# Lag kernels of four state-space groups on four column parts of TensorE at once, lag zero from b and c themselves, and an earlier bank copy in the MLP

## The chip, the cores and the metric

The kernel runs on one core of a Trainium2 chip (trn2). A core has five engines that work side by side and wait for each other through semaphores: TensorE (PE; its weight loads are shown as a lane of their own, PEld), VectorE (DVE), ScalarE (ACT), GpSimd (POOL) and SyncE (SP), which issues most of the DMA transfers. TensorE writes to PSUM, which has eight banks; VectorE and ScalarE read the banks and so give them back.

The metric is the device time of one execution in microseconds; a kernel's number is the median over several runs. Matmul clock is given as a share of full speed ("granted clock").

## The reference

The reference is one encoder layer on two sequences of 512 tokens with 1024 features:

```
h    = rms_norm(x, ln1);  q, k, v, u, g_att, g_ssm = split(h @ w_in)
y    = windowed attention(q, k, v)
s    = S5(u): 64 groups of 16 channels, 64 complex states per group, two directions
       bu_t = B_bar u_t;  h_t = A_bar h_(t-1) + bu_t;  out_t = Re(C h_t) + d_skip * u_t
s    = gelu(s) * sigmoid(gelu(s) @ w_glu + b_glu)
x    = x + (sigmoid(g_att) * y + sigmoid(g_ssm) * s) @ w_out
out  = x + relu(rms_norm(x, ln2) @ w_up)^2 @ w_down
```

The change touches the S5 branch and the first products of the last line. In S5 the effect of `u` at one token on the output `n` tokens later (a lag of `n`) is the 16x16 matrix Re(C A_bar^n B_bar) of its group; the other direction has the same with negative lags, and lag zero is the sum of both directions plus the diagonal `d_skip`.

## The kernel before

All the large products are made in a split form: each 32-bit operand is cut into a high part (a cast on ScalarE) and a low part (a subtraction on VectorE), and three matmuls stand for one (`mm3`, L114 to L118). The kernel goes through these stages: the projection of `u` and the gates, the S5 tables (this change), a scan over chunks of eight tokens on VectorE, the reading out of S5, attention, the GLU and the output product, the up product of the MLP and the down product of the MLP. The MLP uses seven products of half-size blocks in place of eight.

**The table stage** is the loop `for q in range(NQ4)` (L720 to L746): 16 turns, each for four groups (`SG = 4`); two turns share the operands of eight groups (`SB = 8`). The order of PE, ACT, DVE and SP here is written out by hand (`manual_schedule`, opened at L270), so each engine goes through its instructions as the Python code issues them. A turn issues:

- `coefficients` (L602, in odd turns, for the next two): small VectorE products that make `bb` (B_bar) and two planes for each of `bb` and `cx` (C).
- `lags_out(q - 1)` (L702) and `table_out(q)` (L656): DMA issues on SP. The lag kernels go to `lag_scr` in memory.
- `turn(q, gp)` (L664): four transposes of `bpre` on TensorE into a `tps` bank, and ScalarE's copy `bm` of them; two of these.
- `lag_weights` (L624, in even turns after the first): three ScalarE copies of `bb` into `lbt`, 48 columns a group: 16 for the forward direction, 16 for the backward one, 16 for both.
- `tables(q + 1)` (L647): six VectorE instructions: `complex_table` (L630) makes `bpre` with eight powers and `ctab` with nine (index 8 is the power zero).
- `run(3)`: three steps of a gate's or a column's product on TensorE, nine matmuls of 512 columns ("acc").
- `states(q, gp)` (L672): four matmuls into an `sps` bank, and two ScalarE copies of it into `h`; two of these, with the SP loads `inputs_in` for the next turn.
- `lags(q)` (L684): the lag kernels. Eight calls of TensorE: for each of four groups a real and an imaginary one, 48 columns of weights from `lbt`, 144 moving columns from `ctab` (nine lags of 16 channels). Two groups stand at partitions 0 and 64 of the `lag` bank. ScalarE copies the two halves out (`ks`, L695); GpSimd makes `dg`, a diagonal of `d_skip`, and adds it to lag zero (L698, L700).
- `run(3)` again, nine more matmuls, and what is owed to ScalarE and VectorE from the steps.

After the loop GpSimd's queue spreads `lag_scr` into `toep_scr` (L749), which is loaded again near the end of the scan, and the scan starts (L879), with the rest of the gates' products on TensorE beside it.

**The entry of the MLP** (L1875 to L1948) is also ordered by hand on PE, ACT, DVE and POOL. Four half products of the first two row pairs are made before the front's PSUM pools are closed; the third and fourth are `p1` and `p2` at L1904 and L1905, in two `acc` banks. `first_copy` (L1842) copies `p1` to `u1` on ScalarE, `first_rest` (L1850) adds `p2` to it on VectorE. After `front.close()` the pool `ps_m` takes over all eight banks, and each of its tiles waits for what used its bank before (`reuse_waits="tile"`). Its first product is `p6` of row pair 0, with the operands `made[2]` and `T2`; then come `p7` (`made[3]`, `T3`), `p5` (`made[1]`, `T1`), `p3` (`made[4]`, `B22`) and `p4`. From there on the order is made by the framework's planner, except in the last row pair.

```
    p1 = product(acc(), first[1][0], B11)
    p2 = product(acc(), first[1][1], B21)
    x22c = last.temp("x22")
    S.copy(x22c, x22)
...
    begun[0] = rest0()
    u1 = first_copy(p1)
```

Of the kernel before, what the change touches and what calls it, by code (L numbers as in the profile page):

```python
# [24 lines left out]
KT = D // P  # L25
# [15 lines left out]
CH = 16  # L41
# [23 lines left out]
def hybrid_layer(ctx, tc, x, xT, rel, onehot, early, w_qkv, w_ug, q_gain, k_gain, sink,  # L65
# [26 lines left out]
    y2_scr = dram.tile([GROUPS, CH, T, NSEQ * NCHUNK], F32, name="y2_scr")  # L92
    ct_scr = dram.tile([P, GROUPS // SG, 2, SG, 9 * CH], F32, name="ct_scr")
    toep_scr = dram.tile([T, CH, GROUPS, T * CH], F32, name="toep_scr")
# [89 lines left out]
    cf = coef_cm.__enter__()  # L184
    e2 = cf.tile([P, 9, GROUPS // SG, 2, SG], F32, name="e2")
    b2 = cf.tile([P, T, GROUPS // SG, 2, SG], F32, name="b2")
    e_s = cf.tile([P, 9, GROUPS], F32, name="e_s")
# [3 lines left out]
    dd = cf.tile([48, GROUPS], F32, name="dd")  # L191
    lbt = cf.tile([P, 2, SB, 48], F32, name="lbt")
    ssmb_cm = tc.tile_pool(name="ssmb", bufs=2)
# [79 lines left out]
    with tc.tile_pool(name="xin", bufs=2, reuse_waits="tile") as xin, tc.tile_pool(name="ssmc", bufs=1) as sc:  # L273
# [8 lines left out]
        V.memset(ones, 1.0)  # L282
        V.memset(lbt, 0.0)
        rows, columns, first_w = {}, {}, []

# [41 lines left out]
        bc_tiles = {0: b_and_c(0)}  # L327
        SP.dma_start(dd[32:48, :], d_skip)
        SP.dma_start(bglu_sb, b_glu)
# [215 lines left out]
        for pl, src in ((1, pr), (0, pi)):  # L545
            sv = src.rearrange("p n (q g) -> p n q g", g=SG)
            S.copy(e2[0:64, 0:8, :, pl], sv[0:64, 1:9])
            S.copy(e2[64:128, 0:8, :, pl], sv[64:128, 8:0:-1])
            S.copy(e2[:, 8, :, pl], sv[:, 0])
            S.copy(b2[0:64, :, :, pl], sv[0:64, 7::-1])  # L550
            S.copy(b2[64:128, :, :, pl], sv[64:128, 0:8])
# [43 lines left out]
    if True:  # L595
# [3 lines left out]
        with tc.tile_pool(name="ssmt", bufs=2) as sp:  # L599
            coefs, made, u_in, turned, lag_ks = {}, {}, {}, {}, {}  # L600

# [22 lines left out]
            def lag_weights(c):  # L624
                bb = coefs[c][0]
                S.copy(lbt[0:64, :, :, 0:16], bb[0:64])
                S.copy(lbt[64:128, :, :, 16:32], bb[64:128])
                S.copy(lbt[:, :, :, 32:48], bb)

            def complex_table(out, q, powers, total, planes, first, n):  # L630

                g0, ql = q * SG, slice(q % 2 * SG, (q % 2 + 1) * SG)
                V.tensor_mul(out.rearrange("p r g n c -> p (r g) n c"),
                             powers[:, 0:n, q].rearrange("p n r g -> p (r g) n")[:, :, :, None]
                             .to_broadcast([P, 2 * SG, n, CH]),
                             planes[:, q % 2].rearrange("p r g c -> p (r g) c")[:, :, None, :]
                             .to_broadcast([P, 2 * SG, n, CH]))
                tb = sp.tile([P, SG, 9, CH], F32, tag="tb", name="tb", bufs=1)
# [6 lines left out]
                V.tensor_add(ov, ov, tv[:, None].to_broadcast([P, 2, SG, n * CH]))  # L645

            def tables(q):  # L647

                bb, bk, cx, ck = coefs[q // 2]
                bpre = sp.tile([P, 2, SG, T, CH], F32, tag="bpre", name="bpre", bufs=1)  # L650
                complex_table(bpre, q, b2, b_s, bk, bb[:, 0], T)
                ctab = sp.tile([P, 2, SG, 9, CH], F32, tag="ctab", name="ctab")
                complex_table(ctab, q, e2, e_s, ck, cx[:, 0], 9)
                made[q] = bpre, ctab
# [29 lines left out]
            def lags(q):  # L684
                ks = lag_ks[q] = sp.tile([48, SG, 9, CH], F32, tag="ks", name="ks", bufs=1)
                ctab = made[q][1]
                ps = ps_o.tile([P, 512], F32, tag="po", name="lag")
                for g in range(SH):
                    for ri in range(2):
                        for e in range(2):  # L690
                            i = e * SH + g
                            PE.matmul(ps[e * 64:e * 64 + 48, g * 144:(g + 1) * 144], lbt[:, ri, q % 2 * SG + i, :],  # L692
                                      ctab[:, ri, i].rearrange("p n c -> p (n c)"), start=ri == 0, stop=ri == 1)
                for e in range(2):
                    S.copy(ks[:, e * SH:(e + 1) * SH].rearrange("p g n c -> p (g n c)"), ps[e * 64:e * 64 + 48, 0:SH * 144])  # L695
                g0 = q * SG
                dg = sp.tile([48, SG, CH], F32, tag="dg", name="dg", bufs=1)
                GP.tensor_tensor(dg[32:48], dd[32:48, g0:g0 + SG, None].to_broadcast([16, SG, CH]),  # L698
                                 ident[32:48, None, 32:48].to_broadcast([16, SG, CH]), op=ALU.mult)
                GP.tensor_tensor(ks[32:48, :, 8, :], ks[32:48, :, 8, :], dg[32:48], op=ALU.add)  # L700

            def lags_out(q):  # L702
                ks, gl = lag_ks.pop(q), slice(q * SG, (q + 1) * SG)
                SP.dma_start(lag_scr[:, gl, 8:15, :], ks[0:16, :, 0:7, :])
                SP.dma_start(lag_scr[:, gl, 0:7, :], ks[16:32, :, 1:8, :])
                SP.dma_start(lag_scr[:, gl, 7, :], ks[32:48, :, 8, :])

# [146 lines left out]
    with tc.tile_pool(name="ssmo", bufs=2, reuse_waits="tile") as sp:  # L854
# [54 lines left out]
        def tables_in(q):  # L909
# [5 lines left out]
            SP.dma_start(toep, toep_scr[:, :, g0:g0 + SH].rearrange("t c g n -> (t c) g n"))  # L915
            ctab = sp.tile([P, 2, SH, 9 * CH], F32, tag="ctab", name="ctab_in", bufs=5)
            SP.dma_start(ctab, ct_scr[:, q // 2, :, q % 2 * SH:(q % 2 + 1) * SH, :])
# [924 lines left out]
    def first_copy(p1):  # L1842
        u1 = up1.tile([P, HALF], F32, tag="u1", name="u1")
        S.copy(u1, p1)  # L1844
        return u1
# [60 lines left out]
    x22c = last.temp("x22")  # L1906
    S.copy(x22c, x22)
    V.tensor_sub(sm[2], a11_, a21_)
    V.tensor_sub(last.s11, x22c, x12)
# [9 lines left out]
    begun[0] = rest0()  # L1919
    u1 = first_copy(p1)  # L1920
    last.old_rows(1)
# [235 lines left out]
def layout(inputs):  # L2157
# [3 lines left out]
    def cols(w, n=CB):  # L2161
# [21 lines left out]
        "c_im": a["c_im"][0].transpose(0, 3, 1, 2).reshape(P, GROUPS, CH),  # L2183
        "d_skip": a["d_skip"][0].reshape(GROUPS, CH).T,
        "w_glu": cols(a["w_glu"][0], P),
# [25 lines left out]
```

## Time and profile before

| what | value |
|---|---|
| median of 3 runs | 1455.46 us (1453.98 to 1455.81) |
| the profiled execution | 1454.6 us, of which 1452.6 us are the span of its instructions |
| PE busy | 1438.1 us (99% of the span), 7768 matmul records |
| PEld / DVE / ACT / POOL busy | 85% / 75% / 54% / 13% of the span |
| granted clock of TensorE | 0.999 over the span |

The page of the profile lists busy times, the span in 40 slices, the DMA queues, the chain that ended last and the costliest groups. A 32-bit matmul call that is not in split form leaves two records in the trace, so the eight calls of `lags` are 16 records. Matmuls are pipelined: a record's duration overlaps its neighbour's, and what one costs is read from the distance of starts.

### The profile page before, as it was taken

Reading aid. Unit: us, or ns where it says so; the run is one execution under the profiler, and the core shown is the slowest. Engines: PE = TensorE matmul, PEld = TensorE weight load, DVE = VectorE, ACT = ScalarE, POOL = GpSimd, SP = SyncE. Lnnn points to the kernel's source line nnn. Section 1 sums busy time; section 2 is a strip of 40 time slices with the busy share of each in tenths; the row PEclk is TensorE's granted clock in tenths of the full one; section 3 lists DMA queues with packets and bytes.
Section 4 is the critical chain, followed back from the end, with each engine's and each line's share of the span. In section 5 each row is a group of like instructions: output and inputs, shape, how many; then the busy total and the mean of one; then the engine's idle time right before and its main releaser. Section 6 shows DMA issues by size and latency. Waiting matters only on the chain.

```text
span 1452.6 us, 21571 instructions
## 1 busy us (share of the span) xinstructions
PE 1438.1 (99%) x7768; PEld 1230.4 (85%) x7768; DVE 1086.3 (75%) x1853; ACT 782.8 (54%) x1404; POOL 182.7 (13%) x259
## 2 busy tenths in 40 slices
PE   9999999999999999999999989999999999999998
PEld 7888888889999999988888878888888888888887
DVE  8799979975637999987854897777776588475654
ACT  7788862233427999896432455554554434333332
POOL 2011120000223555471001000000000000000000
PEclk9999999999999999999999999999999999999999
DMA  8455567359922443356852334544443994464441
GB/s 307 124 168 174 165 207 266 103 173 302 300 88 64 120 123 104 110 190 221 264 175 92 133 116 160 159 142 140 153 149 121 332 326 133 157 192 143 128 131 58
DMA packets 130134, 243.86 MB, mean 168 GB/s; under 512 B 16059, under 2 KB 59323, under 8 KB 130028
## 3 DMA queue, kind: packets, MB, share of 16 engines
q1 hardware_dynamic: 105740, 187.39, 41.0%
q10 hardware_dynamic: 21888, 46.15, 8.4%
q0 software_dynamic: 2400, 8.95, 1.8%
q8 instruction: 61, 1.00, 0.3%
q14 instruction: 45, 0.37, 0.1%
HBM read 173.20 MB, written 81.82 MB: 176 GB/s over the span
## 4 chain that ended last, share of the span: by engine, by line
PE 93%; DVE 3%; ACT 1%; DMA 1%; issue 1%; SPq 0%; POOL 0%; ACTq 0%; DVEq 0%
PE bank L117 13%; PE bank L118 13%; PE bank L116 13%; PE acc L142 12%; PE acc L797 9%; PE acc L835 5%; PE acc L116 3%; PE acc L118 3%; PE acc L117 3%; PE po L1172 3%; PE sps L1140 2%; PE tps L1156 2%; PE sps L677 2%; PE sps L942 2%; PE lag L692 1%; PE sps L940 1%
## 5 line engine op out<-in xcount | busy, mean ns | idle before, releaser
L117 PE MATMUL bank<-b_lo,a_hi 128*128 128x512 f32 x440 | 171.4, 390 | 0.5 <-DVE b_lo L2085 0.5
L116 PE MATMUL bank<-b_hi,a_hi 128*128 128x512 f32 x440 | 171.2, 389 | 0.0
L118 PE MATMUL bank<-b_hi,a_lo 128*128 128x512 f32 x440 | 171.2, 389 | 0.0
L2084 ACT CAST a_hi<-d_a 128x1024 fp32r<-128x1024 f32 x55 | 58.0, 1054 | 177.5 <-PE bank L117 176.2
L2085 DVE TENSOR_TENSOR a_lo<-d_a,a_hi 128x1024 fp32r<-128x1024 f32 x55 | 67.2, 1222 | 98.6 <-ACT a_hi L2084 96.5
L116 PE MATMUL bank<-act,u_hi 128*128 128x512 f32 x256 | 100.3, 392 | 4.7 <-ACT u L1844 4.7
L117 PE MATMUL bank<-act,u_hi 128*128 128x512 f32 x256 | 100.3, 392 | 0.0
L118 PE MATMUL bank<-act,u_lo 128*128 128x512 f32 x256 | 100.2, 391 | 0.0
L117 PEld LDWEIGHTS bank<-b_lo,a_hi 128*128 128x128 f32 x440 | 82.6, 188 | 18.4 <-DVE b_lo L2085 1.2
L118 PEld LDWEIGHTS bank<-b_hi,a_lo 128*128 128x128 f32 x440 | 82.6, 188 | 17.2
L116 PEld LDWEIGHTS bank<-b_hi,a_hi 128*128 128x128 f32 x440 | 82.6, 188 | 17.1
L797 PE MATMUL acc<-w_hi,hT 128*128 128x256 f32 x384 | 84.4, 293 | 0.0
L797 PE MATMUL acc<-w_hi,act 128*128 128x256 f32 x384 | 81.2, 290 | 0.0
L142 PE MATMUL acc<-act,c_hi 128*128 128x512 f32 x256 | 80.6, 395 | 0.0
L142 PE MATMUL acc<-hT,c_hi 128*128 128x512 f32 x256 | 80.5, 394 | 0.0
L1150 ACT ACTIVATE p<-p,nmx 128x257 f32<-128x257 f32 (+1 forms) x128 | 72.0, 564 | 13.0 <-DVE nmx L1144 12.3
L1868 ACT CAST u_hi<-s 128x512 fp32r<-128x512 f32 x64 | 39.7, 622 | 67.2 <-PE bank L117 44.7
L1144 DVE CUSTOM_DVE_ANT_0 p<-sps,bias,nsink 128x256 f32<-128x256 f32 (+1 forms) x128 | 69.3, 542 | 4.4 <-PE sps L1140 2.9
L2085 DVE TENSOR_TENSOR b_lo<-k,b_hi 128x1024 fp32r<-128x1024 f32 x55 | 67.0, 1217 | 0.0
L797 PEld LDWEIGHTS acc<-w_hi,hT 128*128 128x128 f32 x384 | 63.8, 190 | 0.9
L797 PEld LDWEIGHTS acc<-w_hi,act 128*128 128x128 f32 x384 | 63.1, 190 | 0.8
L116 PEld LDWEIGHTS bank<-act,u_hi 128*128 128x128 f32 x256 | 48.5, 189 | 15.2 <-ACT u L1844 5.2
(415 smaller groups left out, 3963.5 us busy)
## 6 DMA issues: line engine op xcount, KB each, us to landing
d_a<-a_scr SPq DMA_DIRECT2D x55, 512.0 KB, 3.6
u_raw<-in_w_up_dram SPq DMA_DIRECT2D x32, 512.0 KB, 5.8
a_scr<-t ACTq DMA_DIRECT2D x64, 256.0 KB, 2.1
k<-in_w_down_dram SPq DMA_DIRECT2D x32, 512.0 KB, 5.8
a_scr<-a ACTq DMA_DIRECT2D x48, 256.0 KB, 3.2
c_raw<-in_w_ug_dram SPq DMA_DIRECT2D x44, 256.0 KB, 4.0
ct_scr<-ctab SPq DMA_DIRECT2D x16, 576.0 KB, 3.2
ctab_in<-ct_scr SPq DMA_DIRECT2D x32, 288.0 KB, 4.8
```

Source lines behind the costliest of these rows:

```text
L116: PE.matmul(ps, a[0], b[0], start=first, stop=False)
L117: PE.matmul(ps, a[0], b[1], start=False, stop=False)
L118: PE.matmul(ps, a[1], b[0], start=False, stop=last)
L142: PE.matmul(self.ps[s], self.w[p == 2][:, k, :], hT[s][p == 1][:, k, :], start=i % (3 * KT) == 0, stop=i % (3 * KT) == 3 * KT - 1)
L797: PE.matmul(ps, act[p == 2][:, k, col:col + P], self.w[k // 4][p == 1][:, k % 4, :], start=i == 0, stop=i == 3 * KT - 1)
L835: PE.matmul(self.ps[s], w_g[self.m][p == 2][:, k, :], y_part(s, int(p == 1), k), start=k + p == 0, stop=k == KT - 1 and p == 2)
L1144: V.tensor_tensor_reduce(self.p[:, h, 1:1 + self.nk], self.s[h][:, 0:self.nk], biases[self.j][h][:, b0:b0 + self.nk], -1.0, nsink[:, hh:hh ...
L1150: S.activation(p, p, AF.Exp, bias=self.nmx[:, h:h + 1], scale=-1.0, accum_out=self.sums[:, h, self.qb:self.qb + 1])
L1172: PE.matmul(self.po, vv, self.hl[i][part], start=i + part == 0, stop=i == self.nkb - 1 and part == 1)
L1868: S.copy(hi, src)
L2084: S.copy(hi, src)
L2085: V.tensor_sub(lo, src, hi.bitcast(F32))
```

## The change

Five things are changed.

1. The lag matmuls: `lbt` has 32 columns a group (forward and backward channels interleaved), `ctab` eight powers, so a call has 32 columns of weights and 128 moving columns. The four groups of a turn stand at partitions 0, 32, 64 and 96 of the bank, and the calls go through the four groups inside, real and imaginary part outside. It is eight calls a turn as before.
2. Lag zero: in even turns eight more calls, for all eight groups of two turns, two groups a call: weights `bz` (32 columns, `bb` in another order), 32 moving columns from `cx` and its negated imaginary part `ncx`. VectorE adds the diagonal in one instruction (`kz`), with a mask `same` that GpSimd makes at the start of the kernel and `d_skip` laid out over all partitions. GpSimd's two instructions a turn go.
3. The copies: one ScalarE copy of 128x128 a turn in place of two of 48x288; in `lag_weights` two copies of `bb` into `lbt`, one into `bz`, and the negation `ncx`, in place of three copies.
4. The DMAs: two a turn for the lag kernels, and two more in even turns for lag zero, in place of three a turn; `ct_scr` and its loads are one ninth smaller. `e2`, `e_s` and `ctab` have eight powers in place of nine, and two ScalarE copies into `e2` go.
5. The MLP's entry: `u1 = first_copy(p1)` for row pair 1 is issued right after the copy of `x22`, in place of after `begun[0] = rest0()`.

```diff
-    e2 = cf.tile([P, 9, GROUPS // SG, 2, SG], F32, name="e2")
+    e2 = cf.tile([P, T, GROUPS // SG, 2, SG], F32, name="e2")
...
-    lbt = cf.tile([P, 2, SB, 48], F32, name="lbt")
+    same = cf.tile([P, 32], F32, name="same")
+    lbt = cf.tile([P, 2, SB, 32], F32, name="lbt")
...
+        GP.tensor_tensor(same_v, eye[0], eye[1], op=ALU.add)
+        for n in (2, 3):
+            GP.tensor_tensor(same_v, same_v, eye[n], op=ALU.add)
...
             def lag_weights(c):
                 bb = coefs[c][0]
-                S.copy(lbt[0:64, :, :, 0:16], bb[0:64])
-                S.copy(lbt[64:128, :, :, 16:32], bb[64:128])
-                S.copy(lbt[:, :, :, 32:48], bb)
+                S.copy(lbt[0:64, :, :, 0::2], bb[0:64])
+                S.copy(lbt[64:128, :, :, 1::2], bb[64:128])
+                ncx = minus[c] = sp.tile([P, SB, CH], F32, tag="ncx", name="ncx", bufs=1)
+                S.activation(ncx, coefs[c][2][:, 1], AF.Copy, scale=-1.0)
+                bz = turned_bb[c] = sp.tile([P, 2, SB // 2, CH, 2], F32, tag="bz", name="bz", bufs=1)
+                S.copy(bz, bb.rearrange("p r (e g) c -> p r e c g", g=2))
...
-                complex_table(ctab, q, e2, e_s, ck, cx[:, 0], 9)
+                complex_table(ctab, q, e2, e_s, ck, cx[:, 0], T)
...
-                for g in range(SH):
-                    for ri in range(2):
-                        for e in range(2):
-                            i = e * SH + g
-                            PE.matmul(ps[e * 64:e * 64 + 48, g * 144:(g + 1) * 144], lbt[:, ri, q % 2 * SG + i, :],
-                                      ctab[:, ri, i].rearrange("p n c -> p (n c)"), start=ri == 0, stop=ri == 1)
-                for e in range(2):
-                    S.copy(ks[:, e * SH:(e + 1) * SH].rearrange("p g n c -> p (g n c)"), ps[e * 64:e * 64 + 48, 0:SH * 144])
...
-                GP.tensor_tensor(dg[32:48], dd[32:48, g0:g0 + SG, None].to_broadcast([16, SG, CH]),
-                                 ident[32:48, None, 32:48].to_broadcast([16, SG, CH]), op=ALU.mult)
-                GP.tensor_tensor(ks[32:48, :, 8, :], ks[32:48, :, 8, :], dg[32:48], op=ALU.add)
+                for ri in range(2):
+                    for e in range(SG):
+                        PE.matmul(ps[e * 32:(e + 1) * 32, 0:P], lbt[:, ri, q % 2 * SG + e, :],
+                                  ctab[:, ri, e].rearrange("p n c -> p (n c)"), start=ri == 0, stop=ri == 1)
+                if q % 2 == 0:
+                    bz, cx = turned_bb[q // 2], coefs[q // 2][2]
+                    for ri, c in enumerate((cx[:, 0], minus[q // 2])):
+                        for e in range(SG):
+                            two = slice(2 * e, 2 * e + 2)
+                            PE.matmul(ps[e * 32:(e + 1) * 32, P:P + 32], bz[:, ri, e].rearrange("p c g -> p (c g)"),
+                                      c[:, two].rearrange("p g c -> p (g c)"), start=ri == 0, stop=ri == 1)
+                S.copy(ks, ps[:, 0:P])
+                if q % 2 == 0:
+                    kz = zero[q] = sp.tile([P, 32], F32, tag="kz", name="kz", bufs=1)
+                    V.scalar_tensor_tensor(kz, same, dd[:, q // 2:q // 2 + 1], ps[:, P:P + 32], op0=ALU.mult, op1=ALU.add)
...
     x22c = last.temp("x22")
     S.copy(x22c, x22)
+    u1 = first_copy(p1)
     V.tensor_sub(sm[2], a11_, a21_)
...
     begun[0] = rest0()
-    u1 = first_copy(p1)
     last.old_rows(1)
```

More of the change, by code (lines that the diff above doesn't have):

```diff
@@ L92, in hybrid_layer @@
     y2_scr = dram.tile([GROUPS, CH, T, NSEQ * NCHUNK], F32, name="y2_scr")
-    ct_scr = dram.tile([P, GROUPS // SG, 2, SG, 9 * CH], F32, name="ct_scr")
+    ct_scr = dram.tile([P, GROUPS // SG, 2, SG, T * CH], F32, name="ct_scr")
     toep_scr = dram.tile([T, CH, GROUPS, T * CH], F32, name="toep_scr")
@@ L184, in hybrid_layer @@
     cf = coef_cm.__enter__()
-    e2 = cf.tile([P, 9, GROUPS // SG, 2, SG], F32, name="e2")
+    e2 = cf.tile([P, T, GROUPS // SG, 2, SG], F32, name="e2")
     b2 = cf.tile([P, T, GROUPS // SG, 2, SG], F32, name="b2")
-    e_s = cf.tile([P, 9, GROUPS], F32, name="e_s")
+    e_s = cf.tile([P, T, GROUPS], F32, name="e_s")
     b_s = cf.tile([P, T, GROUPS], F32, name="b_s")
@@ L190, in hybrid_layer @@
     fi = cf.tile([P, GROUPS], F32, name="fi")
-    dd = cf.tile([48, GROUPS], F32, name="dd")
-    lbt = cf.tile([P, 2, SB, 48], F32, name="lbt")
+    dd = cf.tile([P, KT], F32, name="dd")
+    same = cf.tile([P, 32], F32, name="same")
+    lbt = cf.tile([P, 2, SB, 32], F32, name="lbt")
     ssmb_cm = tc.tile_pool(name="ssmb", bufs=2)
@@ L283, in hybrid_layer @@
         V.memset(lbt, 0.0)
+        eye = [ident[:, n:n + 32].rearrange("p (c g) -> p c g", g=2) for n in range(0, P, 32)]
+        same_v = same.rearrange("p (g c) -> p c g", g=2)
+        GP.tensor_tensor(same_v, eye[0], eye[1], op=ALU.add)
+        for n in (2, 3):
+            GP.tensor_tensor(same_v, same_v, eye[n], op=ALU.add)
         rows, columns, first_w = {}, {}, []
@@ L327, in hybrid_layer @@
         bc_tiles = {0: b_and_c(0)}
-        SP.dma_start(dd[32:48, :], d_skip)
+        SP.dma_start(dd, d_skip)
         SP.dma_start(bglu_sb, b_glu)
@@ L546, in hybrid_layer @@
             sv = src.rearrange("p n (q g) -> p n q g", g=SG)
-            S.copy(e2[0:64, 0:8, :, pl], sv[0:64, 1:9])
-            S.copy(e2[64:128, 0:8, :, pl], sv[64:128, 8:0:-1])
-            S.copy(e2[:, 8, :, pl], sv[:, 0])
+            S.copy(e2[0:64, :, :, pl], sv[0:64, 1:9])
+            S.copy(e2[64:128, :, :, pl], sv[64:128, 8:0:-1])
             S.copy(b2[0:64, :, :, pl], sv[0:64, 7::-1])
@@ L599, in hybrid_layer @@
         with tc.tile_pool(name="ssmt", bufs=2) as sp:
-            coefs, made, u_in, turned, lag_ks = {}, {}, {}, {}, {}
+            coefs, minus, turned_bb, made, u_in, turned, lag_ks, zero = {}, {}, {}, {}, {}, {}, {}, {}
             def coefficients(c):
@@ L637, in complex_table @@
                              .to_broadcast([P, 2 * SG, n, CH]))
-                tb = sp.tile([P, SG, 9, CH], F32, tag="tb", name="tb", bufs=1)
+                tb = sp.tile([P, SG, T, CH], F32, tag="tb", name="tb", bufs=1)
                 V.tensor_mul(tb[:, :, 0:n, :],
@@ L651, in tables @@
                 complex_table(bpre, q, b2, b_s, bk, bb[:, 0], T)
-                ctab = sp.tile([P, 2, SG, 9, CH], F32, tag="ctab", name="ctab")
-                complex_table(ctab, q, e2, e_s, ck, cx[:, 0], 9)
+                ctab = sp.tile([P, 2, SG, T, CH], F32, tag="ctab", name="ctab")
+                complex_table(ctab, q, e2, e_s, ck, cx[:, 0], T)
                 made[q] = bpre, ctab
@@ L684, in lags @@
             def lags(q):
[L685 removed]
+                ks = lag_ks[q] = sp.tile([P, T * CH], F32, tag="ks", name="ks", bufs=1)
                 ctab = made[q][1]
                 ps = ps_o.tile([P, 512], F32, tag="po", name="lag")
[L688 to L693 removed]
@@ new lines, in lags @@
+                S.copy(ks, ps[:, 0:P])
+                if q % 2 == 0:
+                    kz = zero[q] = sp.tile([P, 32], F32, tag="kz", name="kz", bufs=1)
+                    V.scalar_tensor_tensor(kz, same, dd[:, q // 2:q // 2 + 1], ps[:, P:P + 32], op0=ALU.mult, op1=ALU.add)
+            def lags_out(q):
+                ks = lag_ks.pop(q)
+                for d, lag, n in ((0, 8, 0), (1, 0, CH)):
+                    SP.dma_start(lag_scr[:, q * SG:(q + 1) * SG, lag:lag + 7, :].rearrange("c g l n -> g c (l n)"),
+                                 ks[d::2, n:n + 7 * CH])
+                if q % 2 == 0:
+                    kz = zero.pop(q)
+                    for d in range(2):
+                        SP.dma_start(lag_scr[:, q * SG + d:q * SG + SB:2, 7, :].rearrange("c g n -> g c n"),
+                                     kz[d::2, d * CH:(d + 1) * CH])
@@ L915, in tables_in @@
             SP.dma_start(toep, toep_scr[:, :, g0:g0 + SH].rearrange("t c g n -> (t c) g n"))
-            ctab = sp.tile([P, 2, SH, 9 * CH], F32, tag="ctab", name="ctab_in", bufs=5)
+            ctab = sp.tile([P, 2, SH, T * CH], F32, tag="ctab", name="ctab_in", bufs=5)
             SP.dma_start(ctab, ct_scr[:, q // 2, :, q % 2 * SH:(q % 2 + 1) * SH, :])
@@ L2183, in layout @@
         "c_im": a["c_im"][0].transpose(0, 3, 1, 2).reshape(P, GROUPS, CH),
-        "d_skip": a["d_skip"][0].reshape(GROUPS, CH).T,
+        "d_skip": a["d_skip"][0].reshape(KT, 4, 2, CH).transpose(1, 3, 2, 0).reshape(P, KT),
         "w_glu": cols(a["w_glu"][0], P),
```

6 lines of the change are left out of this document (removed).

## The prediction

> **What bounds the kernel now**
>
> I read the page first, then who makes TensorE wait, then the two places that the change touches by stretches of time, by their chain and by single instructions. The page says which engine is full:
>
> ```profile
> PE 1438.1 (99%) x7768; PEld 1230.4 (85%) x7768; DVE 1086.3 (75%) x1853; ACT 782.8 (54%) x1404; POOL 182.7 (13%) x259
> ```
>
> TensorE is the bound, so two things can be won: matmul time, and the few waits. The longest of its waits:
>
> ```profile
> PE bank L116 <- ACT u L1844: 4.7, 1, 4.7
> ```
>
> That is the copy which part 5 of the change moves. Now stretches: the table loop, the idle time before the MLP's first product on the new banks, and what follows it. The first two columns are the stretch and its length, then busy time of PE, PEld, DVE, ACT and POOL with counts, then the granted clock.
>
> ```profile
> 66.00:192.00 126.00, 124.52 (x879) 105.57 (x878) 123.52 (x164) 109.76 (x162) 21.11 (x28) 1.00 0.56 175
> 842.60:847.40 4.80, 0.06 (x2) 0.03 (x1) 4.71 (x9) 4.33 (x9) 0.00 (x0) 1.00 0.04 16
> 847.40:851.80 4.40, 4.40 (x12) 3.48 (x13) 4.32 (x8) 3.59 (x7) 0.00 (x0) 0.61 0.11 42
> ```
>
> In the loop VectorE is as full as TensorE (123.5 and 124.5 of 126), and ScalarE has 16 us left. Whatever TensorE wins there must be within VectorE's reach. The third row shows that the idle 4.8 us is paid twice: afterwards the clock stands at 0.61. The chain that ended last, inside the loop (start, length, what):
>
> ```profile
> 105.08 1.78 PE sps L677 x16
> 106.86 1.12 PE lag L692 x16
> 107.98 0.43 PE acc L116
> ...
> 123.14 1.12 PE lag L692 x16
> ...
> 128.64 0.99 ACT bm L670 x2
> 129.66 2.02 PE sps L677 x16
> 131.69 1.12 PE lag L692 x16
> ```
>
> From the lag block at 106.86 to that at 123.14, two turns later, are 16.28 us: a turn is 8.14 us of TensorE without a gap, 1.12 of them the lag block. The next turn takes 8.55, because ScalarE's copy `bm` came late.
>
> **The lag block**
>
> The two matmul groups that matter for it (line, form, count | busy, mean ns):
>
> ```profile
> L677 PE MATMUL sps<-u_sb,bm 128*128 128x128 f32 x256 | 31.5, 276 | 0.7 <-ACT bm L670 0.7
> L692 PE MATMUL lag<-ctab,lbt 128*48 128x144 f32 x256 | 19.0, 291 | 0.0
> ```
>
> The `states` block has 16 records of 128 columns on the whole array in 1.78 us, 0.111 each. At that rate 16 lag records of 144 columns would take 2.00 us, one after another; they take 1.12. So the two column parts run together: 8 rounds of 0.125 are 1.00, and 0.12 is for entering and leaving. A call leaves two records, which share a part and cannot run together; so TensorE reaches past a call's second record to the next call. With four parts I take four at a time: 4 rounds of 0.111 are 0.44, and with the same 0.12 the block is 0.56, **0.56 less in each of 16 turns: -9.0 us**. Starting four parts and weaving four weight loads will not be quite as smooth; I take back 0.04 a turn, +0.6. The bounds: nothing taken back, or two at a time (8 rounds of 0.111, 0.11 less in a turn, -1.8 in all).
>
> Lag zero adds eight calls, 16 records of 32 columns, in each of eight even turns. No row has so few columns. If the time goes with the columns, 4 rounds are a quarter of 0.44, 0.11; if a record costs as much as one of 128 columns, 0.44. Below nothing is excluded, since records are added. I take 0.25, between the two: **+2.0 us** (0.9 to 3.5). The Trainium skill, TensorEngine Tiling (Array Packing), section Performance Considerations, states about 60 cycles of overhead a matmul, so that one column lasts as long as sixty; an estimate from that page is 60/128 of 0.44, or 0.21 a turn, 1.7 in all; the sum would be 0.3 lower. No run so far shows it.
>
> **Beside it in the loop**
>
> VectorE's and ScalarE's rows in the loop:
>
> ```profile
> L645 DVE TENSOR_TENSOR ctab<-ctab,tb 128x1152 f32<-128x1152 f32 x16 | 21.9, 1367 | 0.6
> L633 DVE TENSOR_TENSOR ctab<-e,ck 128x1152 f32<-128x1152 f32 x15 | 20.3, 1351 | 0.0
> L633 DVE TENSOR_TENSOR bpre<-b,bk 128x1024 f32<-128x1024 f32 x15 | 18.7, 1248 | 0.7 <-PE tps L668 0.7
> L645 DVE TENSOR_TENSOR bpre<-bpre,tb 128x1024 f32<-128x1024 f32 x15 | 18.4, 1225 | 0.5
> ...
> L617 DVE SCALAR_TENSOR_TENSOR bk<-bb 128x128 f32<-128x128 f32 x7 | 2.0, 292 | 0.2
> ```
>
> ```profile
> L695 ACT COPY ks<-lag 48x288 f32<-48x288 f32 x32 | 12.6, 395 | 0.5 <-PE tps L668 0.2
> ```
>
> - VectorE: with eight powers `ctab` becomes a twin of `bpre`: 1367 to 1225 and 1351 to 1248 ns, 0.24 a turn, with the small product between them about 0.28, -4.5 in 16 turns. `kz` adds one instruction in eight turns; the nearest row is L617 with four times the columns, 0.29, so at most that, and I take 0.25: +2.0. VectorE ends some 2.5 us earlier.
> - Can TensorE run ahead of it? The last turn's `bpre` and the transposes that need it:
>
> ```profile
> 187.45 1.22 DVE L645 TENSOR_TENSOR bpre<-bpre,tb 128x1024 f32<-128x1024 f32 x1
> 192.31 1.02 PEld L668 LDWEIGHTS tps<-ident,bpre 128*128 128x128 f32 x8
> ```
>
>   `bpre` is done at 188.67, so there are 3.6 us of slack at the end; with the 2.5 won TensorE may come up to 6.1 us earlier to that point. The terms above are -6.4 for the whole loop, -6.0 up to there. It just fits; turns with less slack may pinch. I put +0.3 for that.
> - ScalarE: two copies of 0.395 a turn become one of 128 columns, at most one of the two: -0.4 a turn. In even turns one copy into `lbt` goes, one into `bz` and the negation come, at most 0.4 each: +0.4. ScalarE gets lighter by over 4 us, TensorE's turns shorten as well, so its late `bm` (0.41 in the turn above) may stay or go: -0.5 (0 to -1.5).
> - New waits: the bank `lag` is given back by `ks` and, in even turns, `kz`, which stands on VectorE behind the next turn's tables; behind that wait on TensorE are the next lag block and all after it. `kz` itself waits for matmuls that ended long before VectorE comes to it. A lag block starts over 8 us after the last one and VectorE's tables end well within that; I put nothing, and the 0.25 of `kz` if the cover goes.
> - SP issues two or four DMAs a turn where it had three, 48 either way; behind them stand the loads for the next turn but one step. The ones for lag zero wait for `kz` in place of GpSimd. GpSimd's loop work and two ScalarE copies into `e2` were off the chain; the mask `same` is three small instructions at the start on an engine that is 13% busy. Nothing for these.
>
> The loop: -9.0 + 0.6 + 2.0 + 0.3 - 0.5 = **-6.6 us**. What follows it, the scan beside gate products, is TensorE at full rate and starts as much earlier.
>
> **The bank copy**
>
> ScalarE, TensorE and VectorE at the entry of the MLP:
>
> ```profile
> 840.50 0.58 ACT L1907 COPY x<-sps 128x512 f32<-128x512 f32 x1
> 842.37 0.62 ACT L1868 CAST u_hi<-s 128x512 fp32r<-128x512 f32 x1 [1.29 <-DVE s L1908]
> ...
> 846.73 0.59 ACT L1844 COPY u<-acc 128x512 f32<-128x512 f32 x1 [0.40 <-ACT a L1856]
> ```
>
> ```profile
> 842.24 0.39 PE L118 MATMUL acc<-act,f 128*128 128x512 f32 x1
> 847.37 0.60 PE L116 MATMUL bank<-act,u_hi 128*128 128x512 f32 x1 [4.74 <-ACT u L1844]
> ...
> 851.82 0.40 PE L116 MATMUL bank<-act,u_hi 128*128 128x512 f32 x1
> ...
> 854.55 0.39 PE L116 MATMUL bank<-act,u_hi 128*128 128x512 f32 x1
> ```
>
> ```profile
> 841.05 0.69 DVE L1538 TENSOR_TENSOR act<-tt,act 128x512 fp32r<-128x512 f32 x1
> ...
> 849.22 0.68 DVE L1852 TENSOR_TENSOR a<-acc,u 128x512 f32<-128x512 f32 x1
> ...
> 858.05 0.68 DVE L1869 TENSOR_TENSOR u_lo<-s,u_hi 128x512 fp32r<-128x512 f32 x1
> ```
>
> The move concerns one instruction, without a DMA. In its new place the copy runs from 841.08 to 841.67, in ScalarE's idle 1.29 us; the cast at 842.37 behind it waits for VectorE anyway, so it is paid by nobody. Late next for `p6` is `T2`'s low part, 841.74, still ahead of TensorE, which is free at 842.47. `p6` then takes what `p7` takes now (851.82 to 854.55, 2.73) in place of 4.45 at the low clock, and `p7` starts at 845.20 in place of 851.82: **-6.6 us**. VectorE does not get earlier, so TensorE comes 6.6 us nearer to it: `p3` at 850.7 against the sum at 849.22 + 0.68, and `p7` of pair 1 at 858.8 against a low part ready at 858.73. Both just fit; I put +0.2, **-6.4 us**.
>
> The sum for the profiled execution: 1454.6 - 6.6 - 6.4 = 1441.6. It lies 0.9 under the median, so the median becomes **1442.5 us**.
>
> **The rivals**
>
> - Two at a time. The trace shows reach over one call; four parts need reach over three calls' second records. Then the loop has -1.8 for the block, +0.11 to +0.44 doubled for lag zero (say +4.0), -0.5: +1.7, and with the copy 1450.8. Against it: with two parts no round is lost at all. The Trainium skill, TensorE: Matmul & The Clock Gate, section Part 3: Packing small matmuls — row/col tiling, has matmuls start and end strictly in program order. By that rule a call's second record would hold up the calls behind it. Chance 0.14.
> - VectorE becomes the bound. If the shorter `ctab` wins half (-2.2) and `kz` costs 0.29, the loop's end moves only by its 3.6 slack: 1455.5 - 3.6 - 6.4 = 1445.5. For it: 98% busy; against it: `bpre`'s own rows. Chance 0.09.
> - The wait moves to another bank. The profile does not say which banks `p6` and `p7` take. If one of the first two is that of the second `p2`, TensorE waits till 849.9 for the sum, idle as long as before, and the copy wins nothing: 1455.5 - 6.6 = 1448.9. Against it: today's wait ends with the copy, not with the sum. Chance 0.08.
> - Slower: the four parts run one after another, because four weight loads share one way in. Then a block is 16 x 0.111 + 0.12 = 1.90, 0.78 more in 16 turns, +12.5, lag zero doubled and more, +4: 1455.5 + 16.5 - 6.4 = 1465.6. It decides from a block of about 1.4 us on, where loop and copy cancel. Against it: today's two parts do run together. Chance 0.03.
> - The copy is not late for the reason shown, or both gains go elsewhere, no change: 0.03.
>
> **How the numbers follow**
>
> The forecast has 0.63, its own range 1440 to 1445.5: lag zero at 0.11 and the late copies gone give 1440; lag zero at 0.44 and more pinching 1445. Two more cases are needed for 8 in 10 and lie up to 1448.9; the low end is 1439.5. A difference under 0.2%, 2.9 us, can hardly be told from none here. Faster than that: all but the slow and the unchanged case and a piece of the two-at-a-time case, 0.90; within it 0.06; slower 0.04.
>
> **What would show it**
>
> Right: lag blocks of about 0.6 us in odd and 0.85 in even turns, still 256 records and 128 more of 32 columns; turns of 7.6 and 7.9; no wait of TensorE for L1844 and a clock of 1.00 through the MLP's entry; the loop's last lag block about 6 us earlier. Wrong: lag blocks of 1 us and more, waits of the `tps` transposes for VectorE in many turns, or a new wait behind `p6`.

## The result and the profile after

The changed kernel takes 1440.28 us, median of 4 runs (1440.09 to 1440.49), against 1455.39 us for the kernel before (4 runs, 1453.98 to 1455.81). The ratio is 0.990, 95% interval 0.9885 to 0.9915: 15.1 us less. The profiled execution took 1440.49 us, of which 1438.7 are its span; that of the kernel before took 1454.6 and 1452.6. So 14.1 us of the gain can be looked for in the two traces.

The busy line of the page after:

```profile
PE 1430.2 (99%) x7896; PEld 1224.3 (85%) x7896; DVE 1079.1 (75%) x1861; ACT 773.4 (54%) x1394; POOL 161.4 (11%) x230
```

The 128 added records are there (7896 for 7768), and TensorE is still the engine without gaps. Its longest waits (us in total, times, longest):

```profile
PE tps L460 <- DVE ones L283: 1.1, 1, 1.1
PE tps L676 <- PE acc L118: 1.0, 1, 1.0
PE po L1187 <- ACT ph L1175: 0.6, 1, 0.6
PE sps L685 <- ACT bm L678: 0.6, 2, 0.3
```

The wait of 4.7 us for `u` is gone, and nothing of its size stands in its place. Stretches of the kernel after, with the columns as before: the loop, and twice the MLP's entry.

```profile
66.00:192.00 126.00, 124.45 (x1061) 105.49 (x1061) 118.58 (x173) 109.27 (x164) 0.00 (x0) 1.00 0.55 171
835.00:840.00 5.00, 5.00 (x24) 4.14 (x23) 4.91 (x9) 3.95 (x7) 0.00 (x0) 1.00 0.00 0
840.00:848.00 8.00, 8.00 (x37) 6.63 (x36) 7.13 (x12) 4.26 (x7) 0.00 (x0) 1.00 0.36 95
```

The entry has no idle time and a clock of 1.00. In the same 126 us VectorE is busy 118.6 in place of 123.5, although the faster turns bring more tables into them. TensorE's timeline around two lag blocks, an even and an odd turn:

```profile
105.39 0.64 PE L698 MATMUL lag<-ctab,lbt 128*32 128x128 f32 x16
105.86 0.24 PE L705 MATMUL lag<-cx,bz 128*32 128x32 f32 x8
105.92 0.25 PE L705 MATMUL lag<-ncx,bz 128*32 128x32 f32 x8
106.09 0.50 PE L116 MATMUL acc<-hT,c_hi 128*128 128x512 f32 x1
...
113.09 0.64 PE L698 MATMUL lag<-ctab,lbt 128*32 128x128 f32 x16
113.66 0.50 PE L116 MATMUL acc<-act,c_hi 128*128 128x512 f32 x1
```

From the block's first start to the next product's start are 0.70 us in the even turn and 0.57 in the odd one; the chain before had 1.12. Inside the odd block the 16 records start in four fours: each four within 0.02 us, the last record 0.37 after the first (before: eight pairs, 0.90). Turns without a stall, counted from one lag block's start to the next, take 7.6 to 7.7 us in place of 8.14.

For the experiments the loop's length is needed apart from what comes ahead of it, since the start of the program differs by up to a microsecond from one execution to another. The products `sps` have one line in all kernels; from their first start to their last are 15 turns and the last turn's `states` block (line, records, ns least/median/most, first and last start in us). Before, then after:

```profile
L677 PE MATMUL sps<-u_sb,bm x256: 270/275/377, 72.3 to 197.6; 128*128 128x128 f32 x128
```

```profile
L685 PE MATMUL sps<-u_sb,bm x256: 270/275/377, 72.6 to 190.8; 128*128 128x128 f32 x128
```

125.3 and 118.2 us: 7.1 less, and 0.54 more for the last turn's lag block, which lies behind.

### The profile page after: what moved, and what is told of

The parts are those of the page before. It is cut to its first block, busy times and chain, and to the rows that moved or that the text cites. A ratio compares the mean times of both kernels' runs of the same rounds, so it can differ in the third digit from the quotient of the medians.

```text
span 1438.7 us, 21754 instructions
## 1 busy us (share of the span) xinstructions
PE 1430.2 (99%) x7896; PEld 1224.3 (85%) x7896; DVE 1079.1 (75%) x1861; ACT 773.4 (54%) x1394; POOL 161.4 (11%) x230
## 3 DMA queue, kind: packets, MB, share of 16 engines
q8 instruction: 62, 1.02, 0.3%
## 5 line engine op out<-in xcount | busy, mean ns | idle before, releaser
L1180 DVE TENSOR_TENSOR pl<-tps,ph 128x512 fp32r<-128x512 f32 x80 | 55.0, 688 | 4.5 <-ACT ph L1175 2.8
```

What stands on the lines that cost most here:

```text
L1180: V.tensor_sub(pl, self.pt[i], self.hl[i][0].bitcast(F32))
```

## The experiments

**The two parts by themselves.** First the lag part without the copy's move, and the other way round.

```
 # first: the kernel after, its copy put back
-    u1 = first_copy(p1)
     V.tensor_sub(sm[2], a11_, a21_)
...
     begun[0] = rest0()
+    u1 = first_copy(p1)
```

> The kernel after, with the bank copy back in its old place, so that the lag part stands alone. Theory (the copy's move is worth 6.6 us, because TensorE's idle 4.7 us and the low clock behind it come back): 1440.3 + 6.6 = 1446.9 us, with a wait of TensorE for u of about 4.7 us and p6 at a low clock. Rival (the MLP's entry would have been mended by the earlier loop alone): about 1440 us.

Measured: 1447.93 us, ratio to the kernel before 0.9948 (0.9935 to 0.9962). The wait and p6 in its trace:

```profile
PE bank L116 <- ACT u L1859: 4.7, 1, 4.7
```

```profile
841.37 0.64 PE L116 MATMUL bank<-act,u_hi 128*128 128x512 f32 x1 [4.74 <-ACT u L1859]
...
845.80 0.39 PE L116 MATMUL bank<-act,u_hi 128*128 128x512 f32 x1
```

The twelve products of p6 take 4.43 us again. Loop: 73.2 to 191.3, 118.1 us, that of the kernel after. The rival falls: the copy needed its move whatever the loop did.

```
 # second: the kernel before, its copy moved
+    u1 = first_copy(p1)
     V.tensor_sub(sm[2], a11_, a21_)
...
     begun[0] = rest0()
-    u1 = first_copy(p1)
```

> The kernel before, with the bank copy moved ahead and nothing else. Theory: 1455.4 - 6.6 = 1448.8 us, no wait for u and a clock of 1.00 through p6. If the two parts add, this run's gain and that of the lag part alone make the whole 15.1 us. Rival (the wait moves to another bank): about 1455 us, with a wait of 4 us or more on p6 or p7 for another releaser.

Measured: 1448.0 us, ratio 0.9952 (0.994 to 0.9965), with the entry full at clock 1.00:

```profile
842.00:847.00 5.00, 5.00 (x24) 4.14 (x23) 4.91 (x9) 3.95 (x7) 0.00 (x0) 1.00 0.00 0
```

The loop is 125.2 us, that of the kernel before. So the parts touch different places, and each is worth 6.8 us (the kernel before took 1454.75 beside both). Together that is 13.6; the 1.5 us up to the 15.1 of the result are no more than the runs of the kernel before differ by (1453.75 to 1456.38).

**The idle time filled.** Is it the idle time that makes p6 slow?

```
     p2 = product(acc(), first[1][1], B21)
+    filler = acc()
+    for i in range(16):
+        PE.matmul(filler, first[1][0][0][:, i % 4, :], B11[0][:, i % 4, :], start=True, stop=True)
```

> The kernel before, with 16 added products of 512 columns into a bank of their own, whose result nobody reads, in the place where TensorE waits 4.74 us for the copy. At the usual 0.23 us each they fill about 3.6 us of that time and cannot make the copy earlier. Theory (the idle time is paid twice, the second time by the low clock afterwards): the idle time shrinks to about 1.1 us, the clock stays at 1.00, p6 takes 2.73 in place of 4.45 us, and the time becomes 1455.4 - 1.7 = 1453.7 us though work is added. Rival (the lower clock after the wait has another cause than the idle time, or costs nothing): 1455.4 us or more, and p6 again takes 4.4 us.

Measured: 1453.26 us, ratio 0.9988 (0.998 to 0.9997), with work added. Timeline, then the stretch of p6, then two waits of this run:

```profile
843.02 3.79 PE L1908 MATMUL acc<-act,f 128*128 128x512 f32 x16
847.95 0.50 PE L116 MATMUL bank<-act,u_hi 128*128 128x512 f32 x1 [1.14 <-ACT u L1844]
...
850.80 0.39 PE L116 MATMUL bank<-act,u_hi 128*128 128x512 f32 x1
```

```profile
847.90:850.70 2.80, 2.75 (x12) 2.30 (x13) 2.71 (x5) 2.56 (x5) 0.00 (x0) 1.00 0.21 78
```

```profile
PE bank L117 <- DVE b_lo L2088: 1.4, 1, 1.4
PE bank L116 <- ACT u L1844: 1.1, 1, 1.1
```

With 1.14 us of idle time p6 takes 2.85 us at clock 1.00; with 4.74 it took 4.45 at 0.61. So 1.6 of the 6.6 us that the copy's move won were the clock. In the profiled execution 0.9 of it is given back further on, where the wait for `b_lo` grew from 0.5 to 1.4. The Trainium skill, TensorE: Matmul & The Clock Gate, Part 1, What's actually happening, has the clock fall to half after an idle window of about 3.4 us. The two idle times, 1.14 and 4.74, lie on either side of that, and the rows agree: the 0.61 is a mean over 4.4 us, and from 847.7 to 851.0 us of the kernel before the clock is 0.50.

**Real and imaginary product of one part next to each other.**

```
-                for ri in range(2):
-                    for e in range(SG):
+                for e in range(SG):
+                    for ri in range(2):
```

The same was done in lag zero. Now all four records of a part stand in the program ahead of the next part.

> The kernel after, with the same matmuls in another order: real and imaginary product of one column part follow each other, then comes the next part, in the lag block and in lag zero. Theory (TensorE starts work of another column part past a record that must wait for its own part): the block stays four at a time, last start about 0.4 us after the first, and the time stays at 1440.3 us, at most 1441. Rival (it reaches past one waiting call at most, or not at all): only two records or one run beside each other, the lag block's starts spread over 0.9 us or more, VectorE covers little of it, and the time is 1447 us (0.44 us more in 16 turns) to 1456 us (1 us more).

Measured: 1440.99 us, ratio 0.9902 (0.9889 to 0.9916); loop 118.4 us.

```profile
105.42 0.26 PE L705 MATMUL lag<-cx,bz 128*32 128x32 f32 x6
105.48 0.20 PE L705 MATMUL lag<-ncx,bz 128*32 128x32 f32 x1
105.49 0.21 PE L705 MATMUL lag<-cx,bz 128*32 128x32 f32 x2
105.51 0.26 PE L705 MATMUL lag<-ncx,bz 128*32 128x32 f32 x7
...
112.72 0.66 PE L698 MATMUL lag<-ctab,lbt 128*32 128x128 f32 x16
113.31 0.50 PE L116 MATMUL acc<-act,c_hi 128*128 128x512 f32 x1
```

The block takes 0.59 us, 0.02 more than in the other order. Its first four records start within 0.04 us of each other, as in the other order, where they belong to four parts; here the first records of the second, third and fourth part stand behind 4, 8 and 12 others in the program. The rows of the lag block do not name the part, so this is read from the pattern. In lag zero the tiles show it: the program has two `cx` and two `ncx` records of each part in turn, and the rows show the first six starts as `cx`. So TensorE starts what another column part has ready, and the order of the calls hardly matters here. The Trainium skill, TensorE: Matmul & The Clock Gate, Part 3: Packing small matmuls — row/col tiling, has matmuls start and end strictly in program order. These rows speak against that for different column parts.

**Two column parts in place of four,** everything else as after (lag zero stays on four).

```
-    lbt = cf.tile([P, 2, SB, 32], F32, name="lbt")
+    lbt = cf.tile([P, 2, SB, 64], F32, name="lbt")
...
-                        PE.matmul(ps[e * 32:(e + 1) * 32, 0:P], lbt[:, ri, q % 2 * SG + e, :],
+                        PE.matmul(ps[e % 2 * 64:e % 2 * 64 + 64, f * P:(f + 1) * P], lbt[:, ri, q % 2 * SG + e, :],
```

> The kernel after, with the lag block on two column parts of 64 columns in place of four of 32 (the weights filled up with zeros to 64 columns, two groups one after the other in each part); lag zero stays on four parts. Same number of records. Theory (the gain is four at a time in place of two): the block's 8 rounds take 0.9 us from first to last start in place of 0.37, about 0.43 us more in each of 16 turns, 6.9 us in all: 1447 us. One copy a turn now has 256 columns and two more transfers a turn are issued, which are beside the path. Rival (the gain comes from the shorter tables of eight powers and the fewer copies, not from the four parts): 1440.5 to 1441.5 us.

Measured: 1448.29 us, ratio 0.9957 (0.9945 to 0.997).

```profile
115.30 1.09 PE L699 MATMUL lag<-ctab,lbt 128*64 128x128 f32 x16
116.32 0.50 PE L116 MATMUL acc<-act,c_hi 128*128 128x512 f32 x1
```

```profile
L685 PE MATMUL sps<-u_sb,bm x256: 270/275/377, 72.5 to 197.9; 128*128 128x128 f32 x128
```

The odd block takes 1.02 us, and the loop 125.4 (0.6 of it one turn's wait for its input), as long as before the change; the time is that of the copy's move alone. Of the 0.54 us that an odd block won by the change, 0.09 belong to the shorter tables (1.118 to 1.024 us, eight rounds of 128 columns in place of 144) and 0.45 to the four parts (1.024 to 0.574). In 15 turns that is 1.4 and 6.8 us. Lag zero's price, 1.0 us in the kernel after, takes most of the 1.4 back, so nearly all of the loop's gain is that four records run together in place of two.

This run is not quite the clean comparison that was meant: an even block is 0.26 us longer than an odd one here, and 0.12 in the kernel after. Ahead of lag zero the block changes from parts of 64 columns to parts of 32, and 0.20 us pass there from one record's start to the next, in place of 0.09.

**Is TensorE still the bound of the loop?** One run takes work from TensorE, one from VectorE, one from both.

```
 # less on TensorE
-                for ri in range(2):
+                for ri in range(1):
 # less on VectorE: complex_table ends behind its second product for ctab
+                if not third:
+                    return
```

> The kernel after, with the imaginary half of the lag products left out (only the real product of each group is computed), so that the lag block has 8 records in place of 16. This takes about 0.23 us a turn from TensorE alone and nothing from VectorE. Theory (TensorE is still the bound of the loop): 16 x 0.23 = 3.7 us less, about 1436.7 us. Rival (VectorE is now the bound): TensorE waits for the tables instead, and the time stays at 1440 us.

> The kernel after, with the third product and its addition left out of the tables of C (the term that joins real and imaginary part), so that VectorE has about 1.9 us less work in each turn and TensorE the same. Theory (TensorE is the bound, VectorE only pinches in a few turns): 0.3 to 0.8 us less, 1439.5 to 1440.0 us. Rival (VectorE is the bound): several us less, 1437 us or lower.

Measured: 1438.73 us (ratio 0.9892, 0.9877 to 0.9908) and 1439.72 us (0.9899, 0.9885 to 0.9912). The times lie too near each other for a verdict, the loops do not. The run with less on TensorE, its rows and two waits in its loop:

```profile
L685 PE MATMUL sps<-u_sb,bm x256: 270/275/377, 72.5 to 189.3; 128*128 128x128 f32 x128
```

```profile
PE tps L676 <- DVE bpre L653: 0.9, 2, 0.5
PE sps L685 <- ACT bm L678: 0.8, 2, 0.6
```

Its blocks are 0.22 us shorter (112.30 to 112.65 in an odd turn), 3.3 us in 15 turns, but the loop is only 1.4 shorter, 116.8 us. TensorE waits for `bpre` and longer for `bm` instead. With less on VectorE the loop is 117.8 us, 0.4 shorter: turn 2, 7.83 us after the change, takes 7.62, and the late turns 10, 11 and 15 stay late (8.24, 7.87, 8.10). That is the theory's amount.

> The kernel after with both earlier cuts: the imaginary half of the lag products is left out, and so are the third product and its addition in the tables of C. The lag products alone took 3.5 us from TensorE's turns, but the time fell by 1.8 us only. Theory (VectorE gave the rest back as waits, so it is nearly as full as TensorE): with VectorE relieved as well the whole 3.5 us and the 0.6 of its pinches come, 1436.2 us, and TensorE waits for no bpre. Rival (the rest went elsewhere, into late copies of ScalarE or loads): 1438 to 1438.7 us.

Measured: 1437.54 us, ratio 0.988 (0.9865 to 0.9895), between both expectations.

```profile
L687 PE MATMUL sps<-u_sb,bm x256: 270/275/377, 73.2 to 188.8; 128*128 128x128 f32 x128
```

```profile
PE sps L687 <- ACT bm L680: 0.8, 2, 0.6
PE tps L678 <- DVE bpre L655: 0.2, 1, 0.2
```

The loop is 115.6 us: 2.6 shorter than after, where 3.7 were free to win. The wait for `bpre` is down to 0.2, and relieving VectorE won 1.2 us here where alone it won 0.4: 0.8 of the 1.9 us that were missing. The late turns 7, 10, 11 and 15 now lose 2.35 us against their neighbours; in the kernel after 10, 11 and 15 lost 1.34. Both reasons were right in part: behind TensorE stand VectorE, and ScalarE's `bm`.

**ScalarE's late turns.** Two tries: the two small copies for lag zero on GpSimd, and the gates' sigmoid behind `bm`.

```
 # first
-                S.activation(ncx, coefs[c][2][:, 1], AF.Copy, scale=-1.0)
+                GP.tensor_scalar(ncx, coefs[c][2][:, 1], -1.0, None, op0=ALU.mult)
...
-                S.copy(bz, bb.rearrange("p r (e g) c -> p r e c g", g=2))
+                GP.tensor_copy(bz, bb.rearrange("p r (e g) c -> p r e c g", g=2))
 # second
                 lags(q)
                 run(3)
-                pay(act_owed)
                 pay(dve_owed)
```

> The kernel after, with the two small copies that lag zero needs (c's negative imaginary part and b turned) made on GpSimd in place of ScalarE. Theory (the stalls that are left at two late turns come from ScalarE's late copy bm, 0.6 us twice): ScalarE gets about 0.7 us lighter in two turns, the late copies go, 0.5 to 1 us less, 1439.5 us. Rival (GpSimd's work beside VectorE makes VectorE slower, or the copies are late for another reason): 1440.3 to 1441.5 us.

Measured: 1440.5 us, ratio 0.9904 (0.989 to 0.9917); loop 118.3 us, unchanged. Turns 11 and 15 are better (7.70 and 7.82), turns 2 and 8 worse (8.15 and 7.99), with 0.7 us of waits for `bpre`. VectorE's second operation on `bk`, after and in this run:

```profile
L623 DVE TENSOR_TENSOR bk<-bb x8: 284/285/286, 64.7 to 173.6; 128x128 f32<-128x128 f32 x8
```

```profile
L623 DVE TENSOR_TENSOR bk<-bb x8: 539/542/549, 64.4 to 174.1; 128x128 f32<-128x128 f32 x8
```

The rival was right in its result: the copies on GpSimd moved the stall from ScalarE to VectorE, whose operation beside them took 542 ns in place of 285.

> The kernel after, with ScalarE's drain of the filler products (the gates' sigmoids among it) at the end of a turn moved behind the next turn's two bm copies; nothing is left out. Theory (the late turns 10, 11 and 15 of the kernel after, 8.24, 7.95 and 8.18 us where their neighbours take 7.62, 7.72 and 7.69, are late because the sigmoid with its table load stands ahead of bm on ScalarE): 0.62 + 0.23 + 0.49 = 1.3 us less, 1439.0 us. Rival (VectorE's tables are as late in these turns as bm): the wait moves to the transposes and the time stays at 1440.3 us.

Measured: 1439.85 us, ratio 0.9895 (0.9879 to 0.9912). ScalarE's timeline ahead of turn 10, first in the kernel after, then here:

```profile
147.55 1.28 ACT L150 ACT_TABLE_LOAD   x1
148.85 0.60 ACT L150 ACTIVATE sg<-acc 128x512 f32<-128x512 f32 x1
149.34 1.07 ACT L678 COPY bm<-tps 128x512 f32<-128x512 f32 x2
```

```profile
147.15 1.08 ACT L678 COPY bm<-tps 128x512 f32<-128x512 f32 x2
...
149.68 1.28 ACT L150 ACT_TABLE_LOAD   x1
150.97 0.60 ACT L150 ACTIVATE sg<-acc 128x512 f32<-128x512 f32 x1
```

Turns 10, 11 and 15 now take 7.61, 7.69 and 7.72; no wait for `bm` is left in the loop, which takes 117.1 us, 1.1 less than after (two other turns, 12 and 14, are 0.1 to 0.2 late). The cause of the late turns is shown: what ScalarE drains of the filler products, a sigmoid in each of these turns, stood ahead of the copies. In the time only 0.4 us of it arrive: in this execution TensorE lost 0.95 us at about 757 us to a piece of the output weights, whose cast waits for its load (0.49 in the profiled execution after, nothing in four of the other runs on the kernel after). What makes that load early or late stays open.

**Lag zero's evacuation off VectorE,** with c's minus sign put into the turned b.

```
+                n = P if q % 2 else P + 32
+                S.copy(ks[:, 0:n], ps[:, 0:n])
...
-                    V.scalar_tensor_tensor(kz, same, dd[:, q // 2:q // 2 + 1], ps[:, P:P + 32], op0=ALU.mult, op1=ALU.add)
+                    GP.tensor_scalar(kz, same, dd[:, q // 2:q // 2 + 1], None, op0=ALU.mult)
+                    GP.tensor_tensor(kz, kz, ks[:, P:P + 32], op=ALU.add)
```

> The kernel after, with lag zero's evacuation taken from VectorE: ScalarE's copy ks takes lag zero's 32 columns along in even turns, and GpSimd makes kz from the copy in two small operations; c's negation is folded into the turned b. Nothing is left out. VectorE then has 8 x 0.24 = 1.9 us less to do and no more idle time in front of kz (2.1 us in three turns). Theory (VectorE pinches TensorE in turns 2 and 11, 0.2 us each, and kz is a part of that): 0.3 to 0.6 us less, 1439.8 us. Rival (these turns are late for ScalarE's or the loads' sake, or GpSimd's operations slow VectorE): 1440.3 to 1441 us.

Measured: 1439.97 us, ratio 0.9897 (0.9882 to 0.9912); loop 118.0 us. Turn 2 still takes 7.80, turn 11 7.87. The gain of 0.2 us in the loop is the size of what such lines differ by; the theory is not confirmed.

**Half as many blocks.** A block costs more than its rounds: an odd block has four rounds of 0.11 us, and TensorE's next product starts 0.57 after its first record; ahead of that record 0.21 us pass, where two `states` records lie 0.11 apart. The last kernel makes the blocks of two turns as one, on top of the two edits above.

```
-                ctab = sp.tile([P, 2, SG, T, CH], F32, tag="ctab", name="ctab")
+                ctab = sp.tile([P, 2, SG, T, CH], F32, tag="ctab", name="ctab", bufs=3)
...
+                for f in range(2):
+                    ctab = made[q - 1 + f][1]
...
-                lags(q)
+                if q % 2:
+                    lags(q)
```

> The kernel with the sigmoids behind bm and lag zero's evacuation off VectorE, and with the lag blocks of two turns made as one, at the end of each odd turn, with a third buffer for the tables of C; nothing is left out. Eight blocks of 8 rounds of lag products and 4 of lag zero stand in place of sixteen. Theory (a block costs TensorE's time not only by its rounds of 0.11 us, but also for entering and leaving the column parts): from the last product ahead of a block to the second behind it an even turn of the kernel after takes 1.242 us and an odd one 1.120, of which 0.34 would pass without a block; one block of both takes 1.242 + 4 x 0.109 = 1.68 in place of 2.02, 0.34 us less in each of 8 pairs, 2.7 us; VectorE's tables take back up to half of it, so 1437.2 to 1438.6 us. Rival (VectorE and ScalarE are so full that TensorE only waits longer for them): 1439.5 us or more, with waits of the transposes for bpre of over 2 us.

Measured: 1437.85 us, ratio 0.9885 (0.9868 to 0.9901), 2.4 us under the kernel after's median.

```profile
111.63 1.08 PE L698 MATMUL lag<-ctab,lbt 128*32 128x128 f32 x32
112.53 0.31 PE L704 MATMUL lag<-cx,bz 128*32 128x32 f32 x16
112.77 0.50 PE L116 MATMUL acc<-act,c_hi 128*128 128x512 f32 x1
```

```profile
L684 PE MATMUL sps<-u_sb,bm x256: 270/275/377, 72.5 to 187.5; 128*128 128x128 f32 x128
```

```profile
PE tps L675 <- DVE bpre L652: 0.5, 2, 0.3
```

The loop takes 115.0 us, 3.2 less than after. But its row ends ahead of the last block, which here holds the work of two turns: from the last `sps` start to the next product are 1.34 us, and 0.78 in the kernel after. With this block it is 2.6 us less; 1.1 and 0.2 belong to the two edits, as measured one at a time, so that 1.4 of the 2.7 us came through.

On TensorE itself the price came out whole. From the last `sps` start to the start of the second product behind it are 0.35 us in a turn without a block and 1.68 in one with the joint block, 2.02 for a pair of turns; in the kernel after it is 1.24 + 1.12 = 2.36. That is the theory's 0.34 us less, and a pair of turns without a stall takes 14.9 to 15.0 us in place of 15.3. So the theory holds: an odd block of the kernel after costs 1.12 - 0.35 = 0.77 us, of which its four rounds of 0.11 are 0.44, and entering and leaving the column parts is a cost of its own, 0.34 us. Late turns took back the rest, the half that the theory had allowed for: TensorE waits 0.5 us for `bpre` and its weight loads 0.9 us for `bm`; how much of the late turns these make stays open. The intervals of this kernel and the kernel after overlap; that it is the faster one rests on the loop's length as much as on the times.

## Why the prediction was right

The forecast was 1442.5 us, the result is 1440.28, with the mechanism as told. Term by term, against the profiled execution, read from the starts of TensorE's products:

| term | predicted | measured |
|---|---|---|
| lag block, 16 turns | -9.0 + 0.6 = -8.4 | 1.118 to 0.574 us, 16 x 0.544 = -8.7 |
| lag zero, 8 turns | +2.0 | 0.698 against 0.574 us, 8 x 0.124 = +1.0 |
| pinches and late `bm` | +0.3 - 0.5 | 0.0 |
| the loop | -6.6 | 15 turns -7.13, last block -0.54: -7.7 |
| the copy | -6.4 | -6.6 |
| not in the sum | 0 | start +0.3, output weights +0.5, `b_lo` -0.4 |
| span | -13.0 | -13.9 |

- **The lag block** was right: four at a time, eight rounds to four. The 0.6 us taken back for weaving was hardly needed. "Two at a time" is refuted by the fours in the trace and, for the reach that it doubted, by the run with the parts in turn.
- **Lag zero** is the one term that was mis-sized, by 1.0 us. Of the two bounds, 0.11 for time that goes with the columns and 0.44 for a record that costs as much as one of 128, the first was nearly exact: four rounds of 32 columns start within 0.11 us, and the turn pays 0.12. The value between them was the wrong choice. The estimate from the Trainium skill, TensorEngine Tiling (Array Packing), Performance Considerations, 0.21 a turn, was nearer than the 0.25, and too high as well: a round of 32 columns took about a quarter of the time of one of 128, and not 60/128 of it.
- **VectorE** is in the bounds given: `kz` takes 244 ns for 0.25, and `ctab` has become the twin of `bpre`:

```profile
L653 DVE TENSOR_TENSOR bpre<-bpre,tb 128x1024 f32<-128x1024 f32 x15 | 18.4, 1225 | 0.5
L653 DVE TENSOR_TENSOR ctab<-ctab,tb 128x1024 f32<-128x1024 f32 x15 | 18.4, 1225 | 0.5
...
L710 DVE SCALAR_TENSOR_TENSOR kz<-same,dd,lag 128x32 f32<-128x32 f32 x8 | 2.0, 244 | 2.1 <-ACT ks L707 2.1
```

  "It just fits" was right: turn 2 is 0.2 us late for VectorE's sake and no other turn as much, and taking 1.9 us a turn from VectorE wins 0.4. One step failed: `kz` does wait, 2.1 us in three turns, where VectorE is ahead of TensorE. No wait of TensorE could be put down to it.
- **ScalarE** got lighter (one `ks` of 266 ns for two of 395), but not where it was late. The prediction's "over 4 us" is not what its own terms add up to, 16 x 0.4 less 8 x 0.4, which is 3.2; the rows give 8.3 us less for `ks` and 2.8 more for the copies in `lag_weights`, 5.5 in all. The stall ahead of turn 7 went, those ahead of 10, 11 and 15 stayed, and turn 2 came: 1.56 us of late turns before, 1.55 after. The -0.5 did not come, since the sigmoid and not the copies was in the way. That the two terms together, -0.2, lie near the measured 0.0 is luck.
- **The bank copy** went as told: it sits in ScalarE's idle time, paid by nobody, and p6 follows p2 without a gap.

```profile
834.07 0.60 ACT L1859 COPY u<-acc 128x512 f32<-128x512 f32 x1
835.47 0.62 ACT L1883 CAST u_hi<-s 128x512 fp32r<-128x512 f32 x1 [0.80 <-DVE s L1924]
```

  The "moves to another bank" and "nothing" cases are refuted by the copy alone, 6.8 us. Both narrow fits behind it held: the 0.2 put aside for them was not needed.
- **The median** was set 0.9 us above the sum for the profiled execution, as it lay before. After, the profiled execution lies 0.2 above its median. These 1.1 us and the 1.1 by which the sum was short make the 2.2. The 1.1 of the median have nothing to do with the mechanism: they hang on which execution was profiled. The result lies at the low end of the forecast's own range, 1440 to 1445.5. The prediction reached that end by lag zero at 0.11 and by late copies that would go; lag zero did cost that little, the late copies stayed, and the offset of the median came in their place.

## What to carry to other kernels

When a small product sits on part of TensorE's array, count its rounds, not its records: halving the rounds won 0.45 us a turn, and with the same tables on two parts in place of four the loop was as long as before the change. Collect such blocks, since entering and leaving the parts cost 0.34 us each time, and ask each time which engine stands next in line, because only 1.4 of a further 3.3 us came through. An idle time of the full engine is worth more than its length when the clock behind it drops: 4.7 us cost 6.6.

## What the runs showed of the hardware

- Matmuls on different column parts start out of program order: with the parts in turn, the first four records of a block start within 0.04 us with up to 12 records ahead of them in the program, and six of lag zero's `cx` records start ahead of the first `ncx`.
- A round of four records costs 0.11 us at 128 columns and about 0.03 at 32, so time went with the columns down to 32.
- A block in column parts between products on the whole array cost 0.34 us beyond its rounds; making two blocks one saved that much in a pair of turns.
- A change from parts of 64 columns to parts of 32 inside a block took 0.20 us from one record's start to the next, in place of 0.09.
- A VectorE operation of 285 ns took 542 beside small GpSimd operations.
